# Down projection of a hybrid decoder layer: two blocks of seven products instead of one

## Chip, cores and metric

The kernel runs on 1 core of one Trainium2 chip. The metric is the device time of one execution in microseconds: the median of several runs.

## The reference, cut to what matters

One decoder layer in float32, 512 tokens of width 1024, with a feed-forward part of width 2816 (22 chunks of 128):

```python
h = rmsnorm(x, g_mix); proj = h @ w_in
y_a = gated_delta_rule(...) @ w_branch_a     # 4 heads, chunks of 64 tokens
y_b = mlstm_chunkwise(...) @ w_branch_b
x = x + (sigmoid(gate_a) * y_a + sigmoid(gate_b) * y_b) @ w_out
h = rmsnorm(x, g_ffn)
x = x + (silu(h @ w1) * (h @ w3)) @ w2
gate = sigmoid(rmsnorm(x, g_ple) @ w_ple_gate)
x = x + gate * (p @ w_ple)
return rmsnorm(x, g_final)
```

## The kernel before

Every float32 operand is split into a high and a low part: `split` lets ACT cast the source to `hi` (L75) and VectorE subtract, `lo = src - hi` (L76). A product is then three matmuls (`mm3`): high by high (L90), and the two mixed ones (L91, L92). Tokens lie in four tiles of 128; `xs` holds the residual stream, one tile of tokens by 1024 columns each.

The stages follow each other: the product `p @ w_ple` at the start (`ple0`, nine warm-up matmuls ahead of it), the input projection and the two mixers, `w_out`, then from about 404 us the second norm (`norm_b`) and the products with w1 and w3 (`proj_b`, `comb`), from 640 us the down projection w2, then the gate (`ple`) and the final norm (`ple_out`).

In the w2 stage, a **plain chunk** is 128 rows of w2 against the matching 128 columns of the gated product (`gg`): `unit` fetches the split weight tile, `lhs2` splits the other operand, `step` multiplies for a token tile, both halves of 512 columns. A **block** takes eight chunks and both column halves as a 2 x 2 block matrix product, in seven products instead of eight (Winograd's form): A11·B11, A12·B21, S1·T1, S2·T2, S4·B22, S3·T3, A22·T4. S and T are sums of the A blocks (made in place in `gg[0]`) and of the B blocks (made in `t1`, `t3` and `rb`). `apart` splits an A block, `bparts` and `bpair` split a B block in two weight tiles. `sprod` is one product for one of the two token tiles of a block row, `tp` = 0 or 1 (called token half below): twelve matmuls of 512 columns, three for each of four 128-row pieces, of which each weight tile holds two. Products share accumulators in PSUM: `pa` takes A11·B11, S2·T2, S3·T3 and A22·T4 in turn, each added onto the last, and is read between them. A result goes into `xs` in two ways: `res` (VectorE adds it, L989) or `res_dma` (ACT copies it to a place in `GT`, L994, and GpSimd issues a DMA that adds it to `xs`, L995).

The order: chunks 8 to 12 plain, the block of chunks 0 to 7, chunks 13 to 18 plain, then the tail, chunks 19 to 21. In the tail the order is by token tile: tile 0 takes chunks 19 and 20 and then 21, the other tiles all three at a time, and after each tile its `res` and its norm (`norm`, with the squares on ACT and the root on GpSimd), whose result `xn` TensorE transposes after tile 2 and 3. The gate's weights (`wpg`, eight units of 128 rows, `wq_unit`) come through the same ring of three raw buffers (`wunit`) as the chunks; units 0 to 2 are fetched and split between plain chunks 14 to 17, unit 3 ahead of the tail, units 4 to 7 in it.

In the w2 stage TensorE, ACT and VectorE run in the order in which the program is written (`manual_schedule`); SP, which issues the loads, and GpSimd are ordered by the scheduler. Each engine does its queue in order.

Of the kernel before, what the change touches and what calls it, by code (L numbers as in the profile page):

```python
# [16 lines left out]
NT = 4  # L17
# [21 lines left out]
def kernel(  # L39
# [934 lines left out]

# [252 lines left out]

    K0, K1, TAIL = 8, 13, 3  # L1230
# [36 lines left out]
    mx = gg[0].rearrange("p (b j) t -> p b j t", j=2)  # L1267
    w2b = w2[0:8 * P, :]
    acount = [0]

    def apart(src):
# [4 lines left out]
        split(hi, lo, src)  # L1276
        return hi, lo

    def load_rb(n):
        for u in (0, 2):  # L1280
            nc.sync.dma_start(rb[:, u:u + 2, 512 * n:512 * n + 512], rows(1, n, w2b)[:, u:u + 2])

    blocks = {}

    def prepare(i):


        if i == 0:
            for u in range(2):
                nc.sync.dma_start(t1[u], rows(0, 0, w2b)[:, 2 * u:2 * u + 2])  # L1290
            for u in (0, 2):
                nc.sync.dma_start(t3[:, u:u + 2], rows(0, 1, w2b)[:, u:u + 2])
            blocks["A11"] = apart(mx[:, :, 0, lo_t])
            V.tensor_tensor(s1, mx[:, :, 1, hi_t], mx[:, :, 0, hi_t], ALU.subtract)
            V.tensor_tensor(mx[:, :, 0, hi_t], mx[:, :, 0, lo_t], mx[:, :, 0, hi_t], ALU.subtract)
        elif i == 1:
            for u in range(2):
                G.dma_start(t1[u], rows(0, 1, w2b)[:, 2 * u:2 * u + 2], accum_op=ALU.add)
            blocks["A12"] = apart(mx[:, :, 1, lo_t])
            V.scalar_tensor_tensor(mx[:, :, 0, lo_t], s1, -1.0, mx[:, :, 0, lo_t], ALU.mult, ALU.subtract)  # L1300
        elif i == 2:
            load_rb(1)
            for u in (0, 2):
                G.dma_start(t3[:, u:u + 2], rows(1, 1, w2b)[:, u:u + 2], accum_op=ALU.add)
            V.scalar_tensor_tensor(mx[:, :, 1, lo_t], mx[:, :, 1, lo_t], -1.0, mx[:, :, 0, lo_t], ALU.mult, ALU.subtract)
            blocks["S1"] = apart(s1)
        elif i == 3:
            load_rb(0)
            blocks["S2"] = apart(mx[:, :, 0, lo_t])
# [10 lines left out]
    B11 = bparts(from_dram(0, w2b))  # L1320
    for t in range(NT):
        step(acc2[t], t, u, False, True)
        res(acc2[t][0], t, 0)
        res_dma(acc2[t][1], t, 1)
        if t == 1:
            B21 = bpair(from_dram(1, w2b), 0)
    A11, A12, S1, S2 = (blocks[n] for n in ("A11", "A12", "S1", "S2"))

    pa = [mm8() for _ in range(2)]
    for tp in range(2):  # L1330
        sprod(pa[tp], tp, A11, B11, True)
    B21 += bpair(from_dram(1, w2b), 2)
    T1 = bparts(lambda u: t1[u // 2])
    for tp in range(2):
        res_dma(pa[tp], tp, 0)
    pc = [mm8() for _ in range(2)]
    for tp in range(2):
        sprod(pc[tp], tp, A12, B21, True)
    for u, t in zip(us, t1):
        V.tensor_tensor(t, t, rb[:, u, 512:], ALU.add)  # L1340
    T2 = bparts(lambda u: t1[u // 2])
    for tp in range(2):
        res(pc[tp], tp, 0)
    pb_ = [mm8() for _ in range(2)]
    for tp in range(2):
        sprod(pb_[tp], tp, S1, T1, True)
    S4 = apart(mx[:, :, 1, lo_t])
    B22 = bparts(lambda u: rb[:, u:u + 2, 512:])
    for tp in range(2):
        res_dma(pb_[tp], 2 + tp, 1, -1)  # L1350
    for u, t in zip(us, t1):
        V.tensor_tensor(rb[:, u, 0:512], rb[:, u, 0:512], t, ALU.add)
    for tp in range(2):
        sprod(pa[tp], tp, S2, T2, False)
    S3 = apart(mx[:, :, 0, hi_t])
    T3 = []
    for tp in range(2):
        T3 += bpair(lambda u: t3[:, u:u + 2], 2 * tp)
        res(pa[tp], tp, 1, -1)
    for tp in range(2):  # L1360
        sprod(pb_[tp], tp, S4, B22, False)
    A22 = apart(mx[:, :, 1, hi_t])
    T4 = []
    for tp in range(2):
        T4 += bpair(lambda u: rb[:, u:u + 2, 0:512], 2 * tp)
        res_dma(pb_[tp], tp, 1, -1)
    for tp in range(2):
        sprod(pa[tp], tp, S3, T3, False)
        res_dma(pa[tp], 2 + tp, 1, -1)
    order += [w2[k * P:(k + 1) * P, :] for k in range(K1, NK)]  # L1370
    preload(0)
    l2 = lhs2(K1, 0)
    for tp in range(2):
        sprod(pa[tp], tp, A22, T4, False)
    preload(1)
    for tp in range(2):
        res(pa[tp], 2 + tp, 0)

    acc2 = [[mm8() for n in range(2)] for t in range(NT)]
    for i, k in enumerate(range(K1, NK - TAIL)):  # L1380
        u = (unit(1), l2)
        l2 = lhs2(k + 1, i + 1)
        for t in range(NT):
            step(acc2[t], t, u, i == 0, False)
        if k == K1 + 1:
            wq_tiles()
        if K1 < k < K1 + 4:
            wq_unit(k - K1 - 1)
    us2 = [(unit(min(1, TAIL - 1 - i)), lhs2(k, k - K1) if i else l2) for i, k in enumerate(range(NK - TAIL, NK))]
# [40 lines left out]
    def ple_out(t, pss):  # L1430
# [105 lines left out]
```

## Time and profile before

| | us |
|---|---|
| median of 3 runs | 811.28 (811.19 to 811.52) |
| the profiled execution | 813.05, of which span 811.3 |
| TensorE busy | 796.5 (98%) |
| VectorE busy | 576.2 (71%) |
| ACT busy | 391.5 (48%) |
| GpSimd busy | 71.6 (9%) |
| mean granted TensorE clock | 0.996 |

The profiled execution is 1.77 us above the median, and 1.75 us of it lie outside the span of its instructions. The times of the trace count from the span's start.

### The profile page before, as it was taken

Reading aid. Unit: us, or ns where it says so; the run is one execution under the profiler, and the core shown is the slowest. Engines: PE = TensorE matmul, PEld = TensorE weight load, DVE = VectorE, ACT = ScalarE, POOL = GpSimd, SP = SyncE. Lnnn points to the kernel's source line nnn. Section 1 sums busy time; section 2 is a strip of 40 time slices with the busy share of each in tenths; the row PEclk is TensorE's granted clock in tenths of the full one; section 3 lists DMA queues with packets and bytes.
Section 4 is the critical chain, followed back from the end, with each engine's and each line's share of the span. In section 5 each row is a group of like instructions: output and inputs, shape, how many; then the busy total and the mean of one; then the engine's idle time right before and its main releaser. Section 6 shows DMA issues by size and latency. Waiting matters only on the chain.

```text
span 811.3 us, 12639 instructions
## 1 busy us (share of the span) xinstructions
PE 796.5 (98%) x4948; PEld 704.9 (87%) x4948; DVE 576.2 (71%) x925; ACT 391.5 (48%) x713; POOL 71.6 (9%) x97
## 2 busy tenths in 40 slices
PE   8999999999999999999999999999999999999996
PEld 6798888888788888888889999999999988887885
DVE  4878799857673435447889998888888748555753
ACT  6557433444562222235775555555555546543432
POOL 2021100102200000002210000000000021100000
PEclk9999999999999999999999999999999999999999
DMA  8434423311135463248771333333337896653121
GB/s 330 168 100 137 111 91 104 93 53 46 34 104 208 142 144 104 102 136 250 152 218 56 128 105 104 104 105 105 106 107 204 261 266 148 154 184 109 53 98 53
DMA packets 45499, 106.98 MB, mean 132 GB/s; under 512 B 8184, under 2 KB 12920, under 8 KB 45440
## 3 DMA queue, kind: packets, MB, share of 16 engines
q1 hardware_dynamic: 40096, 96.21, 36.0%
q0 software_dynamic: 5344, 9.96, 7.1%
q8 instruction: 39, 0.64, 0.3%
q14 instruction: 20, 0.16, 0.1%
HBM read 93.56 MB, written 6.83 MB: 124 GB/s over the span
## 4 chain that ended last, share of the span: by engine, by line
PE 84%; DVE 6%; issue 4%; ACT 2%; POOL 1%; POOLq 0%; DVEq 0%; ACTq 0%
PE c L92 15%; PE c L90 15%; PE c L91 15%; PE mm L90 11%; PE mm L92 11%; PE mm L91 11%; PE c L276 2%; PE pc L90 1%; PE pc L92 1%; PE pc L91 1%; PE c L280 1%; DVE xn L138 1%; DVE wlo L76 0%; DVE hlo L76 0%; POOL rstd L133 0%
## 5 line engine op out<-in xcount | busy, mean ns | idle before, releaser
L76 DVE TENSOR_TENSOR wlo<-raw,whi 128x1024 fp32r<-128x1024 f32 (+1 forms) x90 | 106.7, 1187 | 105.1 <-ACT whi L75 104.5
L75 ACT CAST whi<-raw 128x1024 fp32r<-128x1024 f32 (+1 forms) x90 | 91.9, 1023 | 159.3 <-PE mm L91 65.1
L90 PE MATMUL mm<-hhi,whi 128*128 128x512 f32 (+1 forms) x344 | 133.7, 389 | 0.0
L92 PE MATMUL mm<-hhi,wlo 128*128 128x512 f32 (+1 forms) x344 | 131.5, 382 | 0.0
L91 PE MATMUL mm<-hlo,whi 128*128 128x512 f32 (+1 forms) x344 | 131.5, 382 | 0.0
L92 PEld LDWEIGHTS mm<-hhi,wlo 128*128 128x128 f32 x344 | 64.7, 188 | 12.8
L90 PEld LDWEIGHTS mm<-hhi,whi 128*128 128x128 f32 x344 | 64.7, 188 | 11.8
L91 PEld LDWEIGHTS mm<-hlo,whi 128*128 128x128 f32 x344 | 64.8, 188 | 11.7
L90 PE MATMUL c<-hhi,whi 128*128 128x256 f32 x144 | 40.8, 283 | 0.0
L91 PE MATMUL c<-hlo,whi 128*128 128x256 f32 x144 | 40.7, 283 | 0.0
L92 PE MATMUL c<-hhi,wlo 128*128 128x256 f32 x144 | 40.7, 283 | 0.0
L75 ACT CAST whi<-sv 128x1024 fp32r<-128x1024 f32 x24 | 25.2, 1050 | 28.1 <-PE pc L91 21.3
L92 PE MATMUL c<-whi,g2l 128*128 128x512 f32 x84 | 32.8, 391 | 0.6 <-DVE g2l L76 0.6
L90 PE MATMUL c<-whi,g2h 128*128 128x512 f32 x84 | 33.0, 393 | 0.3 <-ACT g2h L75 0.3
L91 PE MATMUL c<-wlo,g2h 128*128 128x512 f32 x84 | 32.7, 390 | 0.0
L76 DVE TENSOR_TENSOR wlo<-sv,whi 128x1024 fp32r<-128x1024 f32 x24 | 29.3, 1222 | 4.7 <-ACT whi L75 4.7
L91 PEld LDWEIGHTS c<-hlo,whi 128*128 128x128 f32 x144 | 27.6, 192 | 0.0
L92 PEld LDWEIGHTS c<-hhi,wlo 128*128 128x128 f32 x144 | 27.6, 192 | 0.0
L90 PEld LDWEIGHTS c<-hhi,whi 128*128 128x128 f32 x144 | 27.6, 192 | 0.0
L92 PE MATMUL c<-g,wlo 128*128 128x256 f32 x96 | 27.2, 283 | 0.0
L90 PE MATMUL c<-g,whi 128*128 128x256 f32 x96 | 27.2, 283 | 0.0
L91 PE MATMUL c<-g,whi 128*128 128x256 f32 x96 | 27.2, 283 | 0.0
(490 smaller groups left out, 2251.7 us busy)
## 6 DMA issues: line engine op xcount, KB each, us to landing
raw<-in_w_dram SPq DMA_DIRECT2D x58, 512.0 KB, 3.7
raw<-in_wf_dram SPq DMA_DIRECT2D x44, 512.0 KB, 3.4
xs<-GT POOLq DMA_DIRECT2D x22, 256.0 KB, 4.9
raw<-in_wbr_dram SPq DMA_DIRECT2D x8, 512.0 KB, 3.7
raw<-in_wpg_dram SPq DMA_DIRECT2D x8, 512.0 KB, 3.4
gm<-in_x_dram SPq DMA_DIRECT2D x4, 512.0 KB, 7.9
gb<-in_gains_dram SPq DMA_DIRECT2D x4, 512.0 KB, 3.6
pp_dram<-GT SPq DMA_DIRECT2D x8, 256.0 KB, 5.2
```

Source lines behind the costliest of these rows:

```text
L75: S.copy(hi, src)
L76: V.tensor_tensor(lo, src, hi.bitcast(F32), ALU.subtract)
L90: PE.matmul(ps, lhsT=ah, rhs=bh, start=first, stop=False, skip_group_check=more)
L91: PE.matmul(ps, lhsT=ah, rhs=bl, start=False, stop=False, skip_group_check=more)
L92: PE.matmul(ps, lhsT=al, rhs=bh, start=False, stop=last, skip_group_check=more)
L138: V.scalar_tensor_tensor(xn[:, c], xs[:, c], r[:, 0:1], gb[:, c], ALU.mult, ALU.mult)
L276: PE.matmul(ps, lhsT=lhsT, rhs=rhs, start=start, stop=stop)
L280: PE.transpose(ps, src, ident if idn is None else idn)
```

## The change

The w2 stage becomes: chunks 16 to 18 plain, a block of chunks 0 to 7, a block of chunks 8 to 15, the tail of chunks 19 to 21. The two blocks run in one loop; A11, A12 and B11 of the second are prepared during S3·T3 and A22·T4 of the first. B11 and B21 are split from the shared places `t1` and `rb` and no longer through the raw ring; B12 is added into `t1` (by GpSimd's DMA) after B11 was split. In the second block, chunks 19 and 20 are fetched and split ahead of the reads of S3·T3's result, which `res` does; chunk 21 and gate units 0 to 2 ahead of A22·T4. Which of the reads go through `res` and which through `res_dma` changes in several places.

Outside the stage: five more warm-up matmuls after the first three matmuls of `ple0`; `load_w1` in two parts, each within `norm_b` of one token tile; the first two gate products of the feed-forward part inside the loop over `proj_b`, ahead of `comb("T4", ...)`; every second output DMA issued from ACT's queue.

```diff
-    for _ in range(9):
-        PE.matmul(warm[:, 0:P], lhsT=ones, rhs=ones, start=True, stop=True)
+    def fill(n):
+        for _ in range(n):
+            PE.matmul(warm[:, 0:P], lhsT=ones, rhs=ones, start=True, stop=True)
+    fill(9)
...
+            if i == 0 and k == 0:
+                fill(5)
...
+        if mid is not None:
+            load_w1(mid)
         for half, ps in pss.items():
             S.copy(hF[:, half * 4:half * 4 + 4, t * P:(t + 1) * P], ps)
...
-        norm_b(tp, xn[tp])
+        norm_b(tp, xn[tp], mid=tp)
         sprod(pa[tp], tp, A11, T4, False)
-        if tp == 0:
-            load_w1()
...
-        elif i == 2:
-            comb("T4", "B21", "B21", "B22")
-    for f in range(2):
-        g = gslot()
+        if i > 1:
+            f = i - 2
+            g = gslot()
...
+    comb("T4", "B21", "B21", "B22")
...
-    K0, K1, TAIL = 8, 13, 3
+    K0, K1, TAIL = 16, 19, 3
...
+    def split_b11(i):
+        parts = bparts(lambda u: t1[u // 2])
+        for u in range(2):
+            G.dma_start(t1[u], rows(0, 1, w2b[i])[:, 2 * u:2 * u + 2], accum_op=ALU.add)
+        return parts
...
+    for i in range(2):
+        last = i == 1
+        mx = mxs[i]
+        pa = [mm8() for _ in range(2)]
+        for tp in range(2):
+            sprod(pa[tp], tp, A11, B11, True)
+        B21 = split_b21()
+        S1 = apart(s1)
+        T1 = bparts(lambda u: t1[u // 2])
...
+        A22 = apart(mx[:, :, 1, hi_t])
+        T4 = []
+        for tp in range(2):
+            T4 += bpair(lambda u: rb[:, u:u + 2, 0:512], 2 * tp)
+            res_dma(pb_[tp], tp, 1, -1)
+        if not last:
+            load_rb(1, 0)
+            add_t3(1)
+            A11n = apart(mxs[1][:, :, 0, lo_t])
+            sums(mxs[1], rest=False)
+        else:
+            order += [w2[k * P:(k + 1) * P, :] for k in range(K1, NK)]
+            us2 = [(unit(0), lhs2(k, k - K1)) for k in (K1, K1 + 1)]
+        for tp in range(2):
+            sprod(pa[tp], tp, S3, T3, False)
+            (res_dma if not last else res)(pa[tp], 2 + tp, 1, -1)
+        if not last:
+            A12n = apart(mxs[1][:, :, 1, lo_t])
+            sums(mxs[1], first=False)
+            B11n = split_b11(1)
+        else:
+            us2.append((unit(0), lhs2(K1 + 2, 2)))
+            wq_tiles()
+            for c in range(3):
+                wq_unit(c)
+        for tp in range(2):
+            sprod(pa[tp], tp, A22, T4, False)
+            res_dma(pa[tp], 2 + tp, 0)
...
-            nc.sync.dma_start(out[t * P:(t + 1) * P, c], xn[:, c])
+            (nc.scalar if n else nc.sync).dma_start(out[t * P:(t + 1) * P, c], xn[:, c])
```

How this moves instructions, at three places.

VectorE around the last products of the (last) block, before. The rows run from the split of A22's second half (`vt`) over T4's two tiles (from `rb`) to the first plain chunks after the block (`raw`, with `gg` as their other operand). The L989 row is A22·T4's own read; the reads of S3·T3 are not among the rows, since ACT does them there:

```order
L76 TENSOR_TENSOR vt<-gg_3845,vt 128x1024
L76 TENSOR_TENSOR g2l<-rb,g2h 128x1024 x2
L76 TENSOR_TENSOR wlo<-raw,whi 128x1024
L76 TENSOR_TENSOR g2l<-gg_5137,g2h 128x512
L76 TENSOR_TENSOR wlo<-raw,whi 128x1024
L989 SCALAR_TENSOR_TENSOR xs<-c,xs 128x512 x2
L76 TENSOR_TENSOR g2l<-gg_5137,g2h 128x512
L76 TENSOR_TENSOR wlo<-raw,whi 128x1024
L76 TENSOR_TENSOR g2l<-gg_5137,g2h 128x512
```

The same place in the second block after: A22 (`ar`), T4 (`rb`), chunks 19 and 20, the two reads of S3·T3 (L999 is `res`), chunk 21, the four gate units, and the residual add of token tile 0:

```order
L76 TENSOR_TENSOR ar<-gg_5142,ar 128x1024
L76 TENSOR_TENSOR wlo<-rb,whi 128x1024
L76 TENSOR_TENSOR g2l<-rb,g2h 128x1024
L76 TENSOR_TENSOR wlo<-raw,whi 128x1024
L76 TENSOR_TENSOR g2l<-gg_6099,g2h 128x512
L76 TENSOR_TENSOR wlo<-raw,whi 128x1024
L76 TENSOR_TENSOR g2l<-gg_6099,g2h 128x512
L999 SCALAR_TENSOR_TENSOR xs<-c,xs 128x512 x2
L76 TENSOR_TENSOR wlo<-raw,whi 128x1024
L76 TENSOR_TENSOR g2l<-gg_6099,g2h 128x512
L76 TENSOR_TENSOR wq0l<-raw,wq0h 128x1024 x4
L999 SCALAR_TENSOR_TENSOR xs<-c,xs 128x512 x2
```

The reads of S3·T3 now stand behind the splits of two chunks, and three gate units that stood between plain chunks stand in one run ahead of tile 0's residual add.

GpSimd in the w2 stage, before (L1298 is the sum into `t1`, L1304 that into `t3`, L995 the DMA half of `res_dma`):

```order
L995 DMA xs<-GT 128x512 x2
L133 TENSOR_TENSOR rstd<-rstd,nhalf 128x1 x2
L1298 DMA t_6524<-in_w_dram 128x2x512
L1298 DMA t_6525<-in_w_dram 128x2x512
L1304 DMA GT<-in_w_dram 128x2x512 x2
L995 DMA xs<-GT 128x512 x12
L133 TENSOR_TENSOR rstd<-rstd,nhalf 128x1 x4
```

And after (L1307 into `t1`, L1301 into `t3`, L1005 of `res_dma`):

```order
L1301 DMA GT<-in_w_dram 128x2x512
L1005 DMA xs<-GT 128x512 x8
L1301 DMA GT<-in_w_dram 128x2x512 x2
L1005 DMA xs<-GT 128x512 x3
L1307 DMA t_6529<-in_w_dram 128x2x512
L1307 DMA t_6530<-in_w_dram 128x2x512
L1005 DMA xs<-GT 128x512 x11
```

The second block's two sums into `t1` (the second pair of L1307) stand behind all but the last of the first block's reads; before, the only pair stood ahead of all reads of the stage.

ACT at the second norm, before, from the casts of the first token tile's transposes (`hhi`) to the next weight tile (`whi`); `w` are the two units of w1, L966 the copies into `hF`:

```order
L75 CAST hhi<-c 128x4x128 x2
L966 COPY hF<-c 128x4x128 x2
L75 CAST w_3789<-raw 128x1024 x2
L75 CAST hhi<-c 128x4x128 x2
L75 CAST whi<-raw 128x1024
L966 COPY hF<-c 128x4x128 x2
```

After (L974 are the copies into `hF`):

```order
L75 CAST hhi<-c 128x4x128 x2
L75 CAST w_3780<-raw 128x1024
L974 COPY hF<-c 128x4x128 x2
L75 CAST hhi<-c 128x4x128 x2
L75 CAST w_3780<-raw 128x1024
L974 COPY hF<-c 128x4x128 x2
L75 CAST whi<-raw 128x1024 x2
```

One unit's cast moved ahead of the first tile's copies, the other behind the second tile's casts.

## Rows read from the trace of the kernel before

**Rows 1.** The page: busy time by engine; the chain that ended last, by engine

```profile
PE 796.5 (98%) x4948; PEld 704.9 (87%) x4948; DVE 576.2 (71%) x925; ACT 391.5 (48%) x713; POOL 71.6 (9%) x97
PE 84%; DVE 6%; issue 4%; ACT 2%; POOL 1%; POOLq 0%; DVEq 0%; ACTq 0%
```

**Rows 2.** Windows: start:end, length, busy by engine (x count), granted clock, DMA

```profile
10.00:13.00 3.00, 3.00 (x8) 2.30 (x7) 0.85 (x3) 1.78 (x4) 0.56 (x1) 0.50 1.01 412
13.00:16.00 3.00, 3.00 (x17) 2.47 (x16) 1.27 (x2) 2.07 (x5) 0.00 (x0) 1.00 1.06 391
219.00:223.00 4.00, 3.59 (x23) 2.85 (x24) 2.62 (x8) 0.00 (x0) 1.01 (x1) 1.00 0.00 0
420.00:440.00 20.00, 19.76 (x166) 19.59 (x165) 19.53 (x25) 13.17 (x20) 0.98 (x1) 1.00 0.28 95
680.00:700.00 20.00, 20.00 (x90) 16.57 (x89) 14.55 (x14) 9.73 (x13) 4.31 (x5) 1.00 0.45 95
```

**Rows 3.** TensorE's waits, whole run: line <- releaser: us, times, longest

```profile
PE c L280 <- DVE num L764: 1.3, 1, 1.3
PE c L91 <- DVE hlo L76: 0.8, 1, 0.8
PE c L92 <- DVE g2l L76: 0.6, 1, 0.6
PE pc L90 <- DVE gg L1169: 0.2, 1, 0.2
```

**Rows 4.** ACT timeline: start, us, engine, line, op [idle before <- releaser]

```profile
727.37 1.05 ACT L75 CAST whi<-raw 128x1024 fp32r<-128x1024 f32 x1 [3.87 <-PE c L92]
732.81 1.05 ACT L75 CAST whi<-raw 128x1024 fp32r<-128x1024 f32 x1 [3.87 <-PE c L92]
```

**Rows 5.** Timelines: TensorE at the stretch's ends, VectorE in the tail

```profile
640.06 0.40 PE L90 MATMUL c<-whi,g2h 128*128 128x512 f32 x1
...
758.58 0.47 PE L92 MATMUL mm<-wq0h,h3l 128*128 128x512 f32 x1
...
743.14 1.37 DVE L989 SCALAR_TENSOR_TENSOR xs<-c,xs 128x512 f32<-128x512 f32 x2 [0.23 <-PE c L92]
...
746.62 1.41 DVE L138 SCALAR_TENSOR_TENSOR xn<-xs,rstd,gb 128x512 f32<-128x512 f32 x2 [0.74 <-POOL rstd L133]
```

**Rows 6.** ACT timeline in S3·T3

```profile
697.46 0.60 ACT L994 ACTIVATE GT<-c 128x512 f32<-128x512 f32 x1 [2.17 <-PE c L92]
```

**Rows 7.** VectorE timeline, three operations one behind another

```profile
691.00 0.69 DVE L989 SCALAR_TENSOR_TENSOR xs<-c,xs 128x512 f32<-128x512 f32 x1
691.61 1.22 DVE L76 TENSOR_TENSOR vt<-gg,vt 128x1024 fp32r<-128x1024 f32 x1
692.74 1.22 DVE L76 TENSOR_TENSOR g2l<-rb,g2h 128x1024 fp32r<-128x1024 f32 x1
```

**Rows 8.** DMA issues, 600 to 740 us: count, KB each, median us to landing

```profile
raw<-in_wpg_dram SPq DMA_DIRECT2D x5, 512.0 KB, 3.4
```

**Rows 9.** Landing of the accumulating DMAs of L1298 (alone) and L1304 (a pair)

```profile
DMA to landing us min/median/max: 7.5/8.0/8.5
...
DMA to landing us min/median/max: 9.0/10.4/11.8
```

**Rows 10.** The start: the warm-up's group; TensorE's timeline

```profile
L181 PE MATMUL mm<-ones 128*128 128x128 f32 x18 | 4.2, 430 | 1.0 <-POOL nhalf L107 1.0
...
8.55 0.49 PE L90 MATMUL mm<-whi 128*128 128x512 f32 x1 [1.77 <-ACT whi L75]
...
9.63 0.63 PE L92 MATMUL mm<-whi,wlo 128*128 128x512 f32 x1
...
13.03 0.40 PE L91 MATMUL mm<-wlo,whi 128*128 128x512 f32 x1
```

**Rows 11.** The end: SP's and ACT's timelines

```profile
807.38 0.81 SPq L1453 DMA_DIRECT2D out_dram<-xo  x2
...
806.87 0.72 ACT L1450 ACTIVATE xo<-xs,rstd 128x512 f32<-128x512 f32 x1 [0.97 <-POOL rstd L1448]
```

More of the change, by code (lines that the diff above doesn't have):

```diff
@@ L1190 @@
         if j == NP:
-            order += [w2[k * P:(k + 1) * P, :] for k in range(8, 13)]
+            order += [w2[k * P:(k + 1) * P, :] for k in range(16, 19)]
             preload(1)
@@ L1266 @@
     t3 = GT[:, 4:8, :]
[L1267 to L1268 removed]
+    mxs = [gg[i].rearrange("p (b j) t -> p b j t", j=2) for i in range(2)]
+    w2b = [w2[8 * P * i:8 * P * (i + 1), :] for i in range(2)]
     acount = [0]
@@ L1277, in apart, with load_rb @@
         return hi, lo
-    def load_rb(n):
+    def load_rb(i, n):
         for u in (0, 2):
[L1281 to L1293, printed above, removed]
+            nc.sync.dma_start(rb[:, u:u + 2, 512 * n:512 * n + 512], rows(1, n, w2b[i])[:, u:u + 2])
@@ new lines, in load_b11, with load_t3, add_t3 @@
+    def load_b11(i):
+        for u in range(2):
+            nc.sync.dma_start(t1[u], rows(0, 0, w2b[i])[:, 2 * u:2 * u + 2])
+    def load_t3(i):
+        for u in (0, 2):
+            nc.sync.dma_start(t3[:, u:u + 2], rows(0, 1, w2b[i])[:, u:u + 2])
+    def add_t3(i):
+        for u in (0, 2):
+            G.dma_start(t3[:, u:u + 2], rows(1, 1, w2b[i])[:, u:u + 2], accum_op=ALU.add)
+    def split_b11(i):
+        parts = bparts(lambda u: t1[u // 2])
+        for u in range(2):
+            G.dma_start(t1[u], rows(0, 1, w2b[i])[:, 2 * u:2 * u + 2], accum_op=ALU.add)
+        return parts
@@ L1294, in prepare, with split_b21, sums @@
+    def split_b21():
+        return bparts(lambda u: rb[:, u:u + 2, 0:512])
+    def sums(mx, first=True, rest=True):
+        if first:
             V.tensor_tensor(s1, mx[:, :, 1, hi_t], mx[:, :, 0, hi_t], ALU.subtract)
             V.tensor_tensor(mx[:, :, 0, hi_t], mx[:, :, 0, lo_t], mx[:, :, 0, hi_t], ALU.subtract)
[L1296 to L1299, printed above, removed]
@@ L1300, in prepare @@
             V.scalar_tensor_tensor(mx[:, :, 0, lo_t], s1, -1.0, mx[:, :, 0, lo_t], ALU.mult, ALU.subtract)
[L1301 to L1304, printed above, removed]
+        if rest:
             V.scalar_tensor_tensor(mx[:, :, 1, lo_t], mx[:, :, 1, lo_t], -1.0, mx[:, :, 0, lo_t], ALU.mult, ALU.subtract)
[L1306 to L1309, printed above, removed]
@@ L1315 @@
             step(acc2[t], t, u, i == 0, False)
-        prepare(i)
+    A11, A12 = (apart(mxs[0][:, :, j, lo_t]) for j in range(2))
+    load_rb(0, 0)
     w_ctx = ExitStack()
@@ L1319 @@
     u = (unit(0), lhs2(K1 - 1, K1 - 1 - K0))
-    B11 = bparts(from_dram(0, w2b))
+    B11 = split_b11(0)
+    load_rb(0, 1)
+    load_t3(0)
+    sums(mxs[0])
     for t in range(NT):
         step(acc2[t], t, u, False, True)
[L1323 to L1377, printed above, removed]
@@ L1379 @@
-    acc2 = [[mm8() for n in range(2)] for t in range(NT)]
[L1380 to L1389, printed above, removed]
+        res_dma(acc2[t][0], t, 0)
@@ new lines @@
+        res(acc2[t][1], t, 1)
+    add_t3(0)
+    for i in range(2):
[8 more added lines that the diff above has]
+        for tp in range(2):
+            res_dma(pa[tp], tp, 0)
+        pc = [mm8() for _ in range(2)]
+        for tp in range(2):
+            sprod(pc[tp], tp, A12, B21, True)
+        S2 = apart(mx[:, :, 0, lo_t])
+        for u, t in zip(us, t1):
+            V.tensor_tensor(t, t, rb[:, u, 512:], ALU.add)
+        T2 = bparts(lambda u: t1[u // 2])
+        for tp in range(2):
+            res_dma(pc[tp], tp, 0)
+        pb_ = [mm8() for _ in range(2)]
+        for tp in range(2):
+            sprod(pb_[tp], tp, S1, T1, True)
+        S4 = apart(mx[:, :, 1, lo_t])
+        B22 = bparts(lambda u: rb[:, u:u + 2, 512:])
+        for tp in range(2):
+            res_dma(pb_[tp], 2 + tp, 1, -1)
+        for u, t in zip(us, t1):
+            V.tensor_tensor(rb[:, u, 0:512], rb[:, u, 0:512], t, ALU.add)
+        if not last:
+            load_b11(1)
+            load_rb(1, 1)
+        for tp in range(2):
+            sprod(pa[tp], tp, S2, T2, False)
+        S3 = apart(mx[:, :, 0, hi_t])
+        T3 = []
+        for tp in range(2):
+            T3 += bpair(lambda u: t3[:, u:u + 2], 2 * tp)
+            res(pa[tp], tp, 1, -1)
+        if not last:
+            load_t3(1)
+        for tp in range(2):
+            sprod(pb_[tp], tp, S4, B22, False)
+        A22 = apart(mx[:, :, 1, hi_t])
+        T4 = []
+        for tp in range(2):
+            T4 += bpair(lambda u: rb[:, u:u + 2, 0:512], 2 * tp)
+            res_dma(pb_[tp], tp, 1, -1)
+        if not last:
+            load_rb(1, 0)
[5 more added lines that the diff above has]
+            us2 = [(unit(0), lhs2(k, k - K1)) for k in (K1, K1 + 1)]
+        for tp in range(2):
+            sprod(pa[tp], tp, S3, T3, False)
+            (res_dma if not last else res)(pa[tp], 2 + tp, 1, -1)
+        if not last:
+            A12n = apart(mxs[1][:, :, 1, lo_t])
[6 more added lines that the diff above has]
+                wq_unit(c)
+        for tp in range(2):
+            sprod(pa[tp], tp, A22, T4, False)
+            res_dma(pa[tp], 2 + tp, 0)
+        if not last:
+            A11, A12, B11 = A11n, A12n, B11n
```

23 lines of the change are left out of this document (13 added, 10 removed).

## The prediction

> **What bounds the kernel now.** I read the page's head first [rows 1]: TensorE is busy in 98% of the span and carries 84% of the chain that ended last. So an edit pays if it takes matmuls out or closes a TensorE gap, and costs if it opens one. The w2 stage (640 to 738 us) has no gap: 90 matmuls per 20 us at the upper clock, in a stretch of its block as elsewhere in it [rows 2]. All other gaps are small; those the edits touch stand in [rows 3].
>
> I measure w2 in units. One chunk of 128 rows of w2, or one product of a block, is 24 matmuls of 512 columns; two neighbouring chunk casts, each released by TensorE, are 5.44 us apart [rows 4]. In a product, TensorE works on token half 0, then 1 (2.72 us each), in each on the first weight tile for 1.36 us, then the second. Before: 5 + 7 + 6 + 3 = 21 units; after: 3 + 7 + 7 + 3 = 20. From its first matmul, 640.06, to the third gate matmul, 758.58 [rows 5], the stretch takes 118.52 us.
>
> **The unit removed.** -5.44 us of TensorE, for certain. What comes back decides.
>
> **A new wait before the last A22·T4.** With E the end of S3·T3 in the second block: A22·T4 adds onto the two banks `pa` that S3·T3 has filled, so it cannot start before these were read into `xs`. Before, ACT did that read, at 697.46, while TensorE worked on the second half [rows 6]. After, VectorE does it, and the order shows the splits of chunks 19 and 20 ahead of it. The cast of chunk 19 needs the tile that holds T3's first half, free at E - 1.36; with 0.2 for the edge and the 1.05 us cast, VectorE starts its split at E - 0.07. The cast of chunk 20 needs T3's second tile, free at E; it is done by E + 1.3, before VectorE comes to it. From then on VectorE alone sets the time: 1.14, 0.60, 1.14, 0.60 from start to start of the four splits where one follows another at once (a split of 1024 columns 1.14, an operation of 512 columns 0.60 [rows 7]), then 0.68 for the read and 0.06 to TensorE. A22·T4 starts at S = E - 0.07 + 4.22 = E + 4.15. Nothing hides this; the next product is this one, and chunk 19 needs the same queue.
>
> **The tail.** Chunk 21's cast waits for T4's first tile, free at S + 4.08, and its split ends at S + 6.6. Only then is a raw buffer free for the third gate-weight unit; issue to landing is 3.4 us [rows 8], so S + 10.0. Behind it on ACT stand its cast, two copies of `pa` and the fourth unit's cast (1.05 + 1.1 + 1.05), and on VectorE the fourth split, ending near S + 14.1, ahead of token tile 0's residual add. Before, all but one of these four units lay between plain chunks. From that add to xn is 746.62 - 743.14 = 3.48 [rows 5], and half of xn another 0.6: S + 18.2. TensorE, after one more unit, tile 0 (4.08), tile 1 (4.08) and half of tile 2 (2.04), wants it at S + 15.64: a wait of 2.6, and 2.2 for the second xn in the same way. The gate's third matmul follows the add by 758.58 - 743.14 = 15.44, so S + 29.5. The wait for chunk 21's split (0.6 [rows 3]) goes, since A22·T4 now covers the splits.
>
> Sum of the stage: 16 units to E (87.04) + 4.15 + 29.5 = 120.7 against 118.52: **+2.2**, though a unit less.
>
> **The second block's T1.** B12 is added into `t1` by GpSimd's DMA after B11 was split, one product ahead, at 54.4 and 55.6 us of the stage (VectorE's splits on 5.44 us units); S1·T1 wants the second half at 66.9. The cast and split take 2.3 us, so the landing must be by 64.5, and the two sums and two splits for T2 behind it want about 64. Such a DMA lands 7.5 to 8.5 us after issue alone, 9.0 to 11.8 as a pair in a busy stretch [rows 9]; the second issue thus lands at 63.1 to 67.4. The wait is 0 to 3.4 us; this is a pair in a quieter stretch, between the two rows, so 64.9: **+1.0**. The first block's place is far earlier, with slack.
>
> **The clock after the new idle.** A stall of 1.77 us near 8.55, after thin work, was followed by a granted clock of 0.50 from 10 to 13 us (the lower level, 1.2 GHz); the clock was back at 1.00 from 13 [rows 2]. Nine matmuls, 9.63 to 13.03, took 3.40 where 9 x 0.227 = 2.04 [rows 10]: 1.36 lost. But 1.35 us of idle at 219.41 was followed by a clock of 1.00 [rows 2, 3]. 4.15 us lies beyond both; it is nearer the first, so I take **+1.4** after S; bounds 0 and 2.8 (again in the tail's waits).
>
> The Trainium skill ("TensorE: Matmul & The Clock Gate", section "Why this matters for your kernels") warns that one long idle stretch of TensorE between bursts puts it back to the lower clock. By the row at 219 alone the sum would be 1.4 us less; by that rule it is as I take it. The row at 8.55 agrees with the rule; no row of this kernel has an idle stretch as long as the one to come.
>
> **Startup.** The five dummy matmuls lie in the 1.77 us idle. At the warm-up's rate (18 entries in 4.21 us for nine [rows 10]) they take 2.3, at most 0.5 beyond where it ended; the next stretch is fed by loads anyway. If they hold the clock, the 1.36 stays: **-1.4**; bounds 0 (the clock falls all the same) and -1.7.
>
> **Middle.** ACT's two casts of w1 no longer stand together ahead of the second tile's casts: the first is done before, the second after. TensorE's 0.8 at 413.27 [rows 3] should go. The gate's first product moves ahead of the T4 combination, three VectorE operations earlier, so the 0.24 at 439.84 goes too. VectorE is nearly full there (19.53 of 20 [rows 2]), so what is saved may come back: **-0.8**, bounds 0 and -1.0.
>
> **End.** The last two output DMAs are issued on one queue at 807.38, 0.81 for both [rows 11]. Split on two queues, one may leave 0.4 earlier, but ACT's own copy ends only at 807.59: **-0.2**, bounds -0.4 and +0.3.
>
> **The rest** at nothing: sums in one run and reads swapped between ACT and VectorE lie beside products of 5.44 us, in which VectorE is busy for 14.55 of 20 us [rows 2]; were this cover gone, each 1.22 us operation would cost itself. Preparing A11, A12 and B11 of the second block adds some 9 us of VectorE over two products; by the order, B11's first half is split 0.2 us before it is needed, so 0 to 0.5, here 0.
>
> **Sum.** +2.2 + 1.0 + 1.4 - 1.4 - 0.8 - 0.2 = +2.2. The profiled execution took 813.05, span 811.3; it would take 815.25. The median of the runs is 811.28, 1.77 lower: 811.28 + 2.2 = **813.5 us**.
>
> **Rivals.** (1) The clock holds through the 4.15 us: +0.8, 812.1. For it: 219.41. Against it: three times its length.
> (2) The change pays. If chunks 19 and 20 find free tiles and their splits lie before E, the read starts when S3·T3's first half ends, and the wait and the clock's fall go: 813.5 - 4.15 - 1.4 = 808.0; with the tail's 2.6 + 2.2 hidden too, 803.2. It decides from where VectorE starts that read before E + 1.0 (no clock lost, and 2.4 us off the wait). Against it stand the order and the rotation of tiles; for it, that I follow these by hand over 100 us.
> (3) The T1 pair lands like the slowest (67.4: +2.4 more) and the clock falls again in the tail (+1.4): 817.3. For it, SP's loads in the same products; against it, the traffic is lighter than where 11.8 was seen.
> (4) The fill saves nothing, since the warm-up's dummies are thin work too: 814.9.
>
> **How the numbers follow.** Chances: forecast 0.38, (1) 0.17, (2) 0.25, (3) 0.12, (4) 0.08. What a measurement tells apart is 0.2%, 1.6 us: 809.7 to 812.9. Faster is (2) and a little of the others' lower bounds: 0.28. Same is (1) and the forecast with a T1 wait near 0: 0.27. Slower: 0.45. The forecast's own range is 811.5 to 816.5; both signs hold much, so the range given reaches into (2): 807.0 to 816.5, leaving out the deeper part of (2) and most of (3).
>
> **What would show it.** After: 20 units of 5.44 us; a TensorE gap of about 4 us released by the residual add on `pa`, some 87 us into the stage, with a clock of 0.5 behind it; two gaps of 2 to 3 us released by xn; one of about 1 us around S1·T1 and S2·T2 of the second block; no clock of 0.5 at 10 to 13 us; none of the waits at 413 and 440. If the gap on `pa` is under 1.7 us, the forecast is wrong by its sign; if the clock behind it stays at 1.00, by 1.4 us.

## The result and the profile after

The changed kernel takes 825.66 us (median of 4 runs, 824.6 to 827.74) where the kernel before takes 811.4 (811.19 to 812.33): a ratio of 1.0172, 95% interval 1.0157 to 1.0188. The forecast was 813.5, its range 807.0 to 816.5; the change costs 14 us where 2 were forecast.

The head of the page, and the chain that ended last by engine, of the changed kernel [rows 1]:

```profile
span 824.1 us, 12680 instructions
...
PE 798.0 (97%) x4934; PEld 703.8 (85%) x4934; DVE 595.6 (72%) x938; ACT 407.0 (49%) x732; POOL 88.8 (11%) x115
...
PE 78%; DVE 7%; DMA 5%; issue 4%; ACT 3%; POOL 2%; SPq 0%; POOLq 0%; ACTq 0%; DVEq 0%
```

TensorE is busy for as long as before (798.0 to 796.5), though a unit of 5.44 us is gone: some of its work ran at the lower clock. And the span has grown by 12.8 us, so it waits 11 us more; "DMA" now stands in the chain. TensorE's waits over the whole run (line <- releaser: us, times, longest) [rows 3]:

```profile
PE c L146 <- DVE xn L138: 4.4, 2, 3.9
PE c L90 <- DVE xs L999: 4.3, 2, 4.1
PE mm L90 <- ACT g2h L75: 2.6, 1, 2.6
PE c L91 <- DVE wlo L76: 1.6, 1, 1.6
...
PE mm L91 <- DVE g2l L76: 0.5, 1, 0.5
```

All five lie in the w2 stage and its tail. They are the read of `pa` ahead of the last A22·T4 (4.1, forecast 4.15), xn in the tail (3.9 and 0.45, forecast 2.6 and 2.2), T1's split and cast (2.6 and 0.5, forecast 1.0 together) and one that was put at nothing, B11's split for the second block (1.6).

The windows of the start and of the three stretches with a low clock (columns as in [rows 2]):

```profile
10.00:13.00 3.00, 3.00 (x14) 2.34 (x13) 0.96 (x3) 2.40 (x6) 0.56 (x1) 1.00 1.02 404
708.00:716.00 8.00, 6.78 (x17) 4.82 (x18) 5.19 (x5) 3.94 (x6) 1.74 (x2) 0.57 0.66 115
738.00:743.00 5.00, 4.45 (x13) 3.55 (x14) 1.00 (x2) 0.00 (x0) 0.00 (x0) 0.66 0.40 122
759.00:764.00 5.00, 4.01 (x15) 3.42 (x16) 4.88 (x6) 1.04 (x2) 0.05 (x1) 0.66 0.58 213
```

The clock of 0.50 at the start [rows 2] is gone, as forecast; but it falls behind each of the three long waits, not behind one. Of the stretches' 8, 5 and 5 us, 3.4, 1.7 and 1.7 are not granted (length times what the clock lacks to 1.00); less what TensorE idles in them, its work takes some 5.7 us longer. How much of that the kernel's time feels is told by the experiment with dummies.

Between the same two matmuls as [rows 5] (the ends of the stretch):

```profile
638.70 0.40 PE L90 MATMUL c<-whi,g2h 128*128 128x512 f32 x1
```

```profile
771.04 0.46 PE L92 MATMUL c<-wq0h,h3l 128*128 128x512 f32 x1
```

The stretch takes 132.34 us (before 118.52): +13.82, made up of -5.44 for the unit, +13.4 in the gaps named, -0.9 for gaps of before that are gone (0.30 and 0.61), +5.7 by the clock, and 1.1 in pauses under 0.2. It begins 1.36 earlier than before, and from its end to the span's end there are 0.34 more: 13.82 - 1.36 + 0.34 = 12.8.

Two rows from inside the stretch, the first matmul of S1·T1 in the second block and the first transposes of xn in the tail:

```profile
708.75 0.79 PE L90 MATMUL mm<-g2h,ar 128*128 128x512 f32 x1 [2.64 <-ACT g2h L75]
```

```profile
759.99 1.08 PE L146 MATMUL c<-cst_sb,xn 128*128 128x128 f32 x4 [3.93 <-DVE xn L138]
```

Where T1's wait comes from is told by the chain, in order of time (start, us, what):

```profile
681.04 10.53 DMA GT<-in_w_dram
...
691.85 1.21 POOL GT L1301
...
695.61 12.03 DMA t<-in_w_dram
707.65 1.05 ACT g2h L75
...
708.73 1.24 DVE g2l L76
```

T3's load for the second block lands 10.53 us after its issue. GpSimd's queue has the sum into `t3` (L1301), which needs it, ahead of the sums into `t1`; only behind that and three DMAs of `res_dma`, at 695.61, is the first of these issued, and it takes 12.03 to land. (B11's own splits, at 693.85 to 696.2 on VectorE, would have let it go hardly earlier: both queues were late.) The landings of the pair of sums into `t3` (L1301) and of the pair into `t1` (L1307), both of the second block, as in [rows 9], and GpSimd's issues of the four:

```profile
DMA to landing us min/median/max: 6.1/6.7/7.3
...
DMA to landing us min/median/max: 12.0/12.8/13.7
```

```profile
691.85 1.21 POOL L1301 DMA_DIRECT2D GT<-in_w_dram  x1 [7.12 <-DMA GT<-in_w_dram]
693.22 1.21 POOL L1301 DMA_DIRECT2D GT<-in_w_dram  x1 [0.15 <-issue]
...
695.61 4.00 POOL L1307 DMA_DIRECT2D t<-in_w_dram  x2
```

Two sums into `t3` and two into `t1` are issued within 5 us, on top of the loads: the pair in front lands in 6.1 and 7.3 us, the pair behind it in 12.0 and 13.7, and the two issues of `t1` alone take 4.00 where they took 1.2 each. Forecast were issues at 54.4 and 55.6 us of the stage and 9.3 to the landing of the second; they came at 56.9 and 57.8, and it took 13.7.

VectorE ahead of the last A22·T4 (timeline), and the matmul that waited:

```profile
734.24 1.23 DVE L76 TENSOR_TENSOR wlo<-raw,whi 128x1024 fp32r<-128x1024 f32 x1 [0.59 <-ACT whi L75]
735.38 0.68 DVE L76 TENSOR_TENSOR g2l<-gg,g2h 128x512 fp32r<-128x512 f32 x1
735.98 1.22 DVE L76 TENSOR_TENSOR wlo<-raw,whi 128x1024 fp32r<-128x1024 f32 x1
737.12 0.68 DVE L76 TENSOR_TENSOR g2l<-gg,g2h 128x512 fp32r<-128x512 f32 x1
737.72 1.28 DVE L999 SCALAR_TENSOR_TENSOR xs<-c,xs 128x512 f32<-128x512 f32 x2
```

```profile
738.55 0.47 PE L90 MATMUL c<-whi,ar 128*128 128x512 f32 x1 [4.08 <-DVE xs L999]
```

The four splits stand one behind another, the two reads behind them: the queue that the prediction wrote down, with the durations that it gave.

### The profile page after: what moved, and what is told of

It reads as the page before. It is cut to its first block, busy times and chain, and to the rows that moved or that the text cites. A ratio compares the mean times of both kernels' runs of the same rounds, so it can differ in the third digit from the quotient of the medians.

```text
span 824.1 us, 12680 instructions
## 1 busy us (share of the span) xinstructions
PE 798.0 (97%) x4934; PEld 703.8 (85%) x4934; DVE 595.6 (72%) x938; ACT 407.0 (49%) x732; POOL 88.8 (11%) x115
## 4 chain that ended last, share of the span: by engine, by line
PE 78%; DVE 7%; DMA 5%; issue 4%; ACT 3%; POOL 2%; SPq 0%; POOLq 0%; ACTq 0%; DVEq 0%
PE c L90 13%; PE c L91 13%; PE c L92 13%; PE mm L91 10%; PE mm L90 10%; PE mm L92 10%; PE c L282 2%; DMA t<-in_w_dram 1%; DMA GT<-in_w_dram 1%; PE pc L92 1%; PE pc L91 1%; PE pc L90 1%; PE c L286 1%; DMA gm<-in_x_dram 1%; DMA pp_dram<-GT 1%
## 5 line engine op out<-in xcount | busy, mean ns | idle before, releaser
L76 DVE TENSOR_TENSOR wlo<-raw,whi 128x1024 fp32r<-128x1024 f32 (+1 forms) x80 | 94.4, 1182 | 82.9 <-ACT whi L75 82.1
L75 ACT CAST whi<-raw 128x1024 fp32r<-128x1024 f32 (+1 forms) x80 | 81.4, 1020 | 145.9 <-PE mm L91 65.4
L90 PEld LDWEIGHTS mm<-hhi,whi 128*128 128x128 f32 x344 | 64.7, 188 | 11.8
L1005 POOL DMA_DIRECT2D xs<-GT x36 | 36.9, 1194 | 74.3 <-ACT GT L1004 61.6
L1301 POOL DMA_DIRECT2D GT<-in_w_dram x4 | 4.9, 1213 | 230.1 <-DMA xs<-x_dram 220.5
L90 PE MATMUL c<-g,whi 128*128 128x256 f32 x96 | 27.3, 284 | 0.4 <-ACT GT L1206 0.4
L448 DVE SCALAR_TENSOR_TENSOR acc<-pre,prm_sb,acc 128x512 f32<-128x512 f32 x36 | 26.9, 747 | 0.5
L90 PE MATMUL c<-hhi,g2h 128*128 128x256 f32 x96 | 27.2, 283 | 0.0
L91 PE MATMUL c<-hlo,g2h 128*128 128x256 f32 x96 | 27.2, 283 | 0.0
```

The source lines that it names most:

```text
L75: S.copy(hi, src)
L76: V.tensor_tensor(lo, src, hi.bitcast(F32), ALU.subtract)
L90: PE.matmul(ps, lhsT=ah, rhs=bh, start=first, stop=False, skip_group_check=more)
L91: PE.matmul(ps, lhsT=ah, rhs=bl, start=False, stop=False, skip_group_check=more)
L448: V.scalar_tensor_tensor(acc, pre[:, j:j + T], cw(j), acc, ALU.mult, ALU.add)
L1005: G.dma_start(xs[:, t, n * 512:(n + 1) * 512], st, accum_op=ALU.add)
```

## The experiments

The experiments compare with runs of the kernel before on the same chip; its median there was 812.0 to 812.5.

**Read first.** In the second block, each read of S3·T3 straight behind its half, chunks 19 and 20 behind the reads.

```diff
-            us2 = [(unit(0), lhs2(k, k - K1)) for k in (K1, K1 + 1)]
+            us2 = []
         for tp in range(2):
             sprod(pa[tp], tp, S3, T3, False)
             (res_dma if not last else res)(pa[tp], 2 + tp, 1, -1)
+            if last:
+                us2.append((unit(0), lhs2(K1 + tp, tp)))
```

> The changed kernel, with the reads of S3·T3's result in the second block put ahead of the splits of chunks 19 and 20 on VectorE (each read straight behind its half). Order theory: the gap of 4.08 us ahead of the last A22·T4 comes from this order alone, and the low clock behind it (738 to 742 us) costs another 1.5; both go, 5 to 5.5 us less than the changed kernel's 825.7, so near 820.5. Rival, VectorE is simply too full at the end of the block: the wait moves on to chunks 19 to 21 in the tail, and no more than 1 us is saved.

820.51 us, 1.0106 (1.009 to 1.0121). The gap and the low clock behind it are gone, and 5.4 us with them by the ratios; xn's gap of 3.7 stays. The order of two rows on VectorE cost this, not VectorE's load. The medians hold other differences too, as the run's one profile tells: T1's wait is 1.35 instead of 2.64, and TensorE waits 1.61 at 406 us, both at places that the edit leaves alone. From S1·T1 to xn's transposes (709.14 to 754.41), where the edit lies, it is 45.3 us instead of 51.2.

**No sum into t1.** The second block's two DMAs that add B12 into `t1` are left out.

```diff
-        for u in range(2):
+        for u in range(2 - 2 * i):
             G.dma_start(t1[u], rows(0, 1, w2b[i])[:, 2 * u:2 * u + 2], accum_op=ALU.add)
```

> The changed kernel without the two DMAs that add B12 into t1 in the second block; this part of the computation is left out. Landing theory: the gaps of 2.64 and 0.47 us at S1·T1 and the low clock behind them (2.9 us lost from 708 to 716) hang on these two landings; 6 us less, near 819.7. Rival, the second block's VectorE work is late by itself: at most 2 us less, the gap stays, now released by a split.

818.8 us, 1.0085 (1.0067 to 1.0104): by the ratios 7 us less. TensorE's rows with a wait in the block are then these two:

```profile
694.66 0.50 PE L91 MATMUL c<-wlo,vt 128*128 128x512 f32 x1 [1.67 <-DVE wlo L76]
...
731.46 0.77 PE L90 MATMUL c<-whi,ar 128*128 128x512 f32 x1 [4.08 <-DVE xs L999]
```

T1's gaps are gone; the split of B11 (1.67) and the read of `pa` (4.08) are as before. So the late landing of these two sums makes the T1 wait, and its whole price is read here: counted from the stage's first matmul (638.10 here, 638.70 in the changed kernel), the last A22·T4 starts at 93.4 us instead of 99.85, 6.5 earlier. The low clock behind that A22·T4 lasts longer than in the changed kernel (3.4 us not granted instead of 1.7), though the wait ahead of it is the same 4.08, and it is 22.5 us to xn instead of 21.4:

```profile
730.00:738.00 8.00, 6.54 (x16) 5.18 (x17) 1.92 (x4) 0.00 (x0) 0.00 (x0) 0.57 0.36 117
```

**B11 first.** B11 of the second block is split right after A11; GpSimd's queue runs in written order, with the sums into `t1` ahead of those into `t3`; T3's load and its sums move into the second block.

```diff
...
-            add_t3(1)
             A11n = apart(mxs[1][:, :, 0, lo_t])
-            sums(mxs[1], rest=False)
...
-            A12n = apart(mxs[1][:, :, 1, lo_t])
-            sums(mxs[1], first=False)
             B11n = split_b11(1)
+            sums(mxs[1], rest=False)
+            A12n = apart(mxs[1][:, :, 1, lo_t])
+            sums(mxs[1], first=False)
```

> The changed kernel with B11 of the second block split right after A11 and ahead of the S sums and A12, and with GpSimd's queue in written order, so that the sums into t1 stand ahead of those into t3 (which now come in the second block). Order theory: B11's split comes 3 to 4 us earlier, the gap of 1.57 us at A11·B11 goes, t1's sums are issued some 5 us earlier and land before S1·T1 wants them, so its gaps and the low clock go too: 7 to 7.5 us less, near 818.5. Rival, the DMA engines are full there (share 1.1 from 695 to 708 us) and t1 lands as late as before: only the 1.57 us, near 824.

820.6 us, 1.0103 (1.0083 to 1.0123). The gaps at A11·B11 and S1·T1 are gone, and the first low clock. A new gap took part of it back (TensorE's timeline):

```profile
722.60 0.47 PE L90 MATMUL c<-whi,ar 128*128 128x512 f32 x1 [1.87 <-DVE xs L999]
```

S3·T3 waits for VectorE's read of `pa`, which stands behind the split of T3, whose sums now come late. The theory holds with that price (7 to 7.5 forecast, 5.6 measured by the ratios); `t1` landed in time. But two things changed at once: the pair was issued 4.8 us earlier (690.77), and it landed in 8.1 and 9.5 us instead of 12.0 and 13.7, as the sums into `t3` were no longer near it. So this run alone does not rule out that the DMA engines were the bound; the last version below does.

**Gate units late.** Gate units 0 to 2 behind tile 0's norm, 3 to 5 behind tile 1's, 6 and 7 behind tile 2's.

```diff
-            wq_tiles()
-            for c in range(3):
-                wq_unit(c)
...
-        if t < 2:
-            wq_unit(4 + 2 * t)
-            wq_unit(5 + 2 * t)
+        for c in ((0, 1, 2), (3, 4, 5), (6, 7), ())[t]:
+            wq_unit(c)
```

> The changed kernel with gate units 0 to 2 no longer ahead of A22·T4 but behind the norm of token tile 0, and units 3 to 7 behind those of tiles 1 and 2. Order theory: tile 0's residual add no longer waits for three units; the gaps of 3.93 and 0.45 us ahead of xn's transposes and the low clock from 760 to 763 (1.4) go: 5 us less, near 820.7. Rival, the gate's weights are then late for the gate's first product and the wait moves there: no more than 1 us is saved.

823.85 us, 1.015 (1.0131 to 1.0168): 1.8 us less by the ratios, nearer the rival. The tail's gap of 3.93 and the clock's fall there are gone, but three others stand in its place:

```profile
762.04 1.23 PE L146 MATMUL c<-cst_sb,xn 128*128 128x128 f32 x8 [0.70 <-DVE xn L138]
...
766.72 0.47 PE L90 MATMUL c<-wq0h,h3h 128*128 128x512 f32 x1 [1.37 <-DVE xs L999]
...
772.47 0.50 PE L91 MATMUL c<-wq1l,h3h 128*128 128x512 f32 x1 [1.07 <-DVE wq1l L76]
```

Three units at a time push tile 1's and tile 2's adds back, and the last units come late for the gate. Where the eight units stand matters as much as that they stand ahead of tile 0.

**Dummies in the waits.** Ten dummy matmuls ahead of S1·T1 of the second block, fifteen ahead of the last A22·T4.

```diff
+        for _ in range(10 * i):
+            PE.matmul(pb_[0][:, 0:P], lhsT=ones, rhs=ones, start=True, stop=True)
         for tp in range(2):
             sprod(pb_[tp], tp, S1, T1, True)
...
+        if last:
+            a0 = [mm8(), mm8()]
+            for _ in range(15):
+                PE.matmul(a0[0][:, 0:P], lhsT=ones, rhs=ones, start=True, stop=True)
         for tp in range(2):
             sprod(pa[tp], tp, A22, T4, False)
...
```

> The changed kernel with dummy matmuls of 128 columns on TensorE inside two of its waits: ten ahead of S1·T1 of the second block, fifteen ahead of the last A22·T4 (on banks that the next product overwrites). Nothing else moves, so the waits stay as long. Clock theory: the low clock behind the two waits (2.9 and 1.5 us lost) does not come, 3 to 4.4 us less than the changed kernel's 825.7 on a like chip, near 822. Rival, the low clock does not follow from the idle time (or what it costs is hidden under the next wait): no change within 0.5 us.

823.5 us, 1.0136 (1.0123 to 1.0149), against 1.0172 of the changed kernel: 2.9 us less, with the waits in place. The same two windows as of the changed kernel:

```profile
708.00:716.00 8.00, 6.43 (x27) 4.48 (x27) 5.43 (x5) 3.94 (x6) 1.75 (x2) 1.00 0.56 98
738.00:743.00 5.00, 4.68 (x21) 3.89 (x22) 0.77 (x2) 0.28 (x1) 0.00 (x0) 1.00 0.36 115
```

The clock stays at 1.00, so the idle time makes it fall. What the two falls cost is told by the same places as in the changed kernel, the starts of S1·T1, of the last A22·T4 and of xn's transposes:

```profile
708.49 0.50 PE L90 MATMUL mm<-g2h,ar 128*128 128x512 f32 x1
...
738.32 0.47 PE L90 MATMUL c<-whi,ar 128*128 128x512 f32 x1 [0.72 <-DVE xs L999]
```

```profile
757.78 1.08 PE L146 MATMUL c<-cst_sb,xn 128*128 128x128 f32 x4 [3.54 <-DVE xn L138]
```

From S1·T1 to A22·T4 it is 29.83 us, as in the changed kernel (29.80) and in "gate units late" (29.82, where the low clock lasted about half as long). At the upper clock TensorE waits there instead, three times 0.76 us for splits and in short pauses: the fall behind T1's wait cost nothing of its own. From A22·T4 to xn it is 19.46 us instead of 21.44: the fall behind the A22·T4 wait cost 2.0. So theory and rival each hold at one of the two places, and the profiles differ by 2.2 us (span 821.9 against 824.1).

**Small edits alone.** The kernel before with one of the other edits each: `fill(5)`; the moves of `load_w1` and of the gates; the output DMA on ACT's queue.

> The kernel before with the five extra warm-up matmuls alone. Clock theory: no granted clock of 0.50 from 10 to 13 us; TensorE reaches the gates' matmul some 1.9 us earlier, as in the changed kernel, and keeps it to the end: 1.4 to 1.9 us less. Rival, a later wait (1.1 at L316, 1.3 at L280) takes it back: no change.

> The kernel before with the two moves in the middle alone (load_w1 in two parts, the first gates ahead of the T4 combination). Prediction's theory: the waits of 0.8 at 413 and 0.2 at 440 go, 0.8 us less. Rival, seen in the changed kernel's trace: VectorE is full from 420 to 440, waits of 0.3 (xn) and 0.4 (the copy of L1206, behind the moved work) appear: 0 to 0.6 us more.

> The kernel before with every second output DMA issued from ACT's queue alone. Prediction's theory: 0.2 us less. Rival, from the changed kernel's trace: from the last matmul to the span's end it is 7.9 us where it was 7.6, so 0.3 us more.

Startup: 811.68 us, 0.9993 (0.9985 to 1.0002). Middle: 812.61, 1.0 (0.9991 to 1.0008). End: 812.51, 1.0002 (0.9993 to 1.001). None tells apart from no change. In the profile, the startup edit's gain is there and lasts to the end: span 809.5 against 811.3, the gates' first matmul at 23.75 where it was at 25.80. Over 11 runs the median shows 0.7 of it. In part this is scatter: the profiles of the other two edits, which leave the start alone, have that matmul at 25.27 and 24.85 and spans of 810.2 and 810.5. The rest stays open.

**Both blocks without the waits.** First the cures together, with the sums into `t3` a product earlier than in "B11 first", the gate units spread (0 and 1; 2 and 3; 4 to 6; 7), the output DMAs on SP.

```diff
...
-            for c in range(3):
+            for c in range(2):
                 wq_unit(c)
...
-        if t < 2:
-            wq_unit(4 + 2 * t)
-            wq_unit(5 + 2 * t)
+        for c in ((2, 3), (4, 5, 6), (7,), ())[t]:
+            wq_unit(c)
```

> The changed kernel with the cures of e1_read_first and e3_b11_first together, the sums into t3 issued one product earlier than in e3 (its new gap of 1.87 us), the gate units two at a time (0 and 1 ahead of A22·T4, 2 and 3 behind tile 0's norm, 4 to 6 behind tile 1's, 7 behind tile 2's), and the output DMAs on SP again. Order theory: the gaps (some 13 us in the w2 stage) and the low clock behind them (some 6) nearly all go; the unit saved and the startup then show: 825.7 - 17 = 808 to 810, below the kernel before. Rival, two blocks side by side load VectorE and the DMA engines beyond what a unit of 5.44 us covers: gaps come back elsewhere, 813 or more.

811.57 us (808.36 to 814.57), 0.9987 (0.9973 to 1.0001), where 808 to 810 were forecast: no gain yet. One large gap was left, ahead of the gate:

```profile
754.29 0.47 PE L90 MATMUL c<-wq0h,h3h 128*128 128x512 f32 x1 [2.36 <-DVE xs L999]
```

Tile 2's add stood behind three gate units. The next version keeps one of them there:

```diff
+        if t == 2:
+            for c in (5, 6, 7):
+                wq_unit(c)
         xn.append(norm(xs[:, t, :], gb))
-        for c in ((2, 3), (4, 5, 6), (7,), ())[t]:
+        for c in ((2, 3), (4,), (), ())[t]:
```

> As x1_waits_out, with gate unit 4 alone behind tile 1's norm and units 5 to 7 behind tile 2's residual adds, ahead of its norm. Order theory: the last large gap of x1 (2.36 us ahead of the gate's first product, released by tile 2's add, which stood behind three gate units on VectorE) and the low clock behind it (1.5) go: 3 us less than x1, 808 to 809, 0.4% below the kernel before on the same chip. Rival: units 5 to 7 are then late for the gate's first product, or VectorE's queue moves the gap to xn: 811 as x1.

806.05 us (804.55 to 808.33), 0.9927 (0.9914 to 0.994): 0.7% faster than the kernel before, and below the 808 to 809 forecast. Not all of the step is the edit's: the version ahead of it had waits of 0.67 and 0.77 at 700 us that this profile lacks, at a place that the edit leaves alone. The head of its page and the windows of the stage's end:

```profile
span 802.8 us, 12680 instructions
...
PE 790.4 (98%) x4934; PEld 700.5 (87%) x4934; DVE 595.0 (74%) x938; ACT 407.7 (51%) x732; POOL 88.6 (11%) x115
```

```profile
700.00:710.00 10.00, 10.00 (x46) 8.29 (x45) 8.15 (x8) 7.17 (x10) 2.16 (x3) 1.00 1.00 182
...
730.00:740.00 10.00, 10.00 (x46) 8.29 (x45) 7.95 (x10) 6.76 (x9) 2.30 (x3) 1.00 0.83 219
740.00:750.00 10.00, 9.96 (x52) 7.91 (x51) 8.05 (x13) 5.16 (x7) 0.55 (x1) 1.00 0.72 210
```

TensorE has no gap left there and keeps its clock. Against the startup edit alone (0.9993) it is 0.66% less, 5.4 us: about the unit that two blocks save, which is there once nothing waits. The stretch from the stage's first matmul to the third gate matmul shows the same, 112.07 us where it was 118.52, that is 5.44 for the unit and the gaps of before (0.9):

```profile
637.09 0.40 PE L90 MATMUL c<-whi,g2h 128*128 128x512 f32 x1
...
749.16 0.39 PE L92 MATMUL c<-wq0h,h3l 128*128 128x512 f32 x1
```

The sums tell why T1 no longer waits. Here GpSimd issues the pair into `t1` at 689.5 and 690.6 and the pair into `t3` behind it, at 693.3 and 694.0, the four within 5 us as in the changed kernel. The landings (the pair of L1307, then that of L1301):

```profile
DMA to landing us min/median/max: 8.2/8.9/9.5
...
DMA to landing us min/median/max: 12.0/12.9/13.8
```

Now `t3`, which is wanted later, has the late landings, and `t1` lands as in "B11 first", where no other sum stood near. So it was not the amount of traffic that made T1 late, but the place of its sums in GpSimd's queue: from it came both the later issue (56.9 us into the stage, here 52.4) and the longer landing.

## Why the prediction was wrong

**The unit removed** (-5.44): right, as the last version shows; the changed kernel hides it.

**The wait before the last A22·T4** (4.15): right in place, cause and size (4.08; read first took it away).

**The tail** (2.6 and 2.2): the cause was right, the split between the two off. The first wait is 3.93: the low clock held up the release of chunk 21's tile (its cast starts 6.0 us behind A22·T4's start, forecast 4.1), and the fourth gate unit's load took 4.70 us; the second then shrinks to 0.45. Together 4.4, forecast 4.8.

**The second block's T1** (+1.0, bounds 0 to 3.4): the step that failed. The last A22·T4 starts 99.85 us into the stage, forecast 92.2 (91.2 + 1.0): 7.7 of the 9.2 us by which the stage misses its forecast with the clock's term (132.3 against 120.7 + 1.0 + 1.4). The landing was weighed between a single DMA's 8.0 and a pair's 10.4, as of a pair in a quieter stretch; the pair took 12.0 and 13.7, behind two sums into `t3`, and the stretch was no quieter (DMA share 1.12 from 695 to 708 us, where the pair before had 1.08 from 648 to 661). And its issue came 2.5 us late: the prediction took B11's splits at 54.4 us without a delay, "0 to 0.5, here 0". But VectorE had no slack in that block (19.5 of 20 us from 680 to 700), the dependent sums took 1.25 from start to start instead of 1.14, and its waits of 0.5 and 0.7 for the first block's T1 may have pushed the queue back. That gap is 1.57. T1's own waits are 3.1, but its price is more: "no sum into t1" shows 6.5 at the start of A22·T4, since the splits and sums behind the late landing keep the next products late as well: from S1·T1 to A22·T4 29.8 us, at either clock, where the forecast had 25.9. With B11's 1.6 that is 8.1 where 1.0 stood, and it is one chain: B11's split, GpSimd's queue, the landing, T1's splits, the sums for T2.

**The clock** (+1.4, bounds 0 and 2.8): right in place and roughly in size. The fall behind the A22·T4 wait was forecast at 1.4 and cost 2.0 ("dummies"). The clock fell behind T1's and xn's waits too, where the sum had nothing. T1's fall cost nothing of its own ("dummies"). xn's cost little as far as the runs show, though none has this wait without a fall: from xn's first transposes to the third gate matmul it is 11.05 us here, with waits of 0.45 and 0.24 that VectorE released, and 11.16 in "read first", where the fall is twice as long and these waits are gone.

The Trainium skill's rule ("TensorE: Matmul & The Clock Gate", section "Why this matters for your kernels") that a long idle stretch puts TensorE back to the lower clock agrees with the falls behind 4.08 and 3.93 us. The fall behind 2.64, like that behind 1.77 at the start, which the prediction read as agreeing, follows a shorter idle stretch than the section warns of; there the measurement decides.

**The rest of the miss** of 12.2 us in all, 7.7 of it T1's: behind A22·T4 the stage takes 1.6 more than forecast, the small edits below give back 1.0 where 2.4 were forecast, and the profiled execution before lay 1.8 above its median where the changed kernel's lies 0.4 above.

**Startup** (-1.4): right in the trace and more, -1.9, as the dummies ran at 1.27 us for ten entries and closed the gap; by the medians of the edit alone no more than 0.7 is seen. **Middle** (-0.8): wrong. The wait at 413 went, but ACT's copy of L1206 now stands behind a cast that waits for VectorE, a combination that the gates were moved ahead of (ACT's timeline, then TensorE's):

```profile
438.52 1.06 ACT L75 CAST vt<-hF 128x1024 fp32r<-128x1024 f32 x1 [3.85 <-DVE hF L1101]
439.48 0.36 ACT L1206 COPY GT<-c 128x256 f32<-128x256 f32 x1
```

```profile
420.96 1.23 PE L967 MATMUL c<-cst_sb,xn 128*128 128x128 f32 x8 [0.29 <-DVE xn L138]
...
439.89 0.39 PE L90 MATMUL c<-g,whi 128*128 128x256 f32 x1 [0.43 <-ACT GT L1206]
```

A TensorE wait of 0.43 took the place of that of 0.24 [rows 3], and one of 0.29 for xn came at 421; alone the two moves change nothing. **End** (-0.2): nothing. ACT's copy ends at 820.03 and its DMA is issued at 820.06, 0.03 behind it, where SP's was issued 0.21 behind the copy (807.80 and 807.59); but it takes 2.47 us to land where SP's took 2.27.

## What to carry to other kernels

An engine that runs its queue in written order turns the place of one row into a wait of its own: before a read that frees an accumulator, write nothing whose inputs are released by the product in progress. Follow a chain through every queue that it crosses, GpSimd's too, since the delay of one link adds to the landing of the next, and price a late input by when the products behind it can run, not by its first wait alone. Where new waits are forecast, ask of each whether the clock lost behind it is felt: here it was where TensorE's own pace set the next start, and hardly where VectorE did. A saving of work on the bounding engine is worth its full size only once no wait is left: with three causes cured one at a time the kernel stayed slower, with all of them it gained about the unit.

## What the runs showed of the hardware

Of four accumulating DMAs of 512 KB that were issued within 5 us, with loads beside them, the two in front landed in 6.1 and 7.3 us (8.2 and 9.5 in the last version) and the two behind in 12.0 and 13.7 (12.0 and 13.8), against 7.5 to 11.8 before [rows 9], and GpSimd needed 4.00 us to issue two of them. The clock fell behind waits of 4.08, 3.93, 2.64 and 2.36 us, in "gate units late" behind one of 1.93 and at the start of the kernel before behind one of 1.77; it stayed at 1.00 behind 1.87 ("B11 first"), 1.57 and 1.35. So between 1.77 and 1.93 us the length of the wait alone did not decide. Behind the same wait of 4.08 a fall took 1.7 us from the clock in the changed kernel and 3.4 in "no sum into t1": its price is not fixed either.
